# A two-layer decoder trunk on one core: 64 instead of 32 tokens by gathered rows, and two thirds of the key blocks in plain fp32

## The chip, the cores and the metric

One Trainium2 chip, one core. The metric is the device time of one execution in microseconds. Engines: TensorE (PE; its weight loads are PEld), VectorE (DVE), ScalarE (ACT), GpSimd (POOL) and SyncE (SP, which issues most DMAs). Each engine works through its own instructions in program order; semaphores tie them together.

## The reference

Two layers, each a token mixer with cross-attention, a norm, and a channel mixer (PEER) with a norm. All of the change lies in the channel mixer, 256 tokens by 1024 columns in fp32, with 16384 experts a layer:

```python
def block(xb):
    q = (xb @ w_q).reshape(n, PEER_HEADS, 2, PEER_HALF)
    s = jnp.einsum('nhpc,pkc->nhpk', q, sk)
    sv, si = lax.top_k(s, PEER_TOPK)                   # 8 heads, 2 halves, 16 of 128
    cand = sv[:, :, 0, :, None] + sv[:, :, 1, None, :]
    cand_id = si[:, :, 0, :, None] * PEER_KEYS + si[:, :, 1, None, :]
    fv, fi = lax.top_k(cand.reshape(n, PEER_HEADS, -1), PEER_TOPK)
    eid = jnp.take_along_axis(cand_id.reshape(n, PEER_HEADS, -1), fi, axis=-1)
    gw = jax.nn.softmax(fv, axis=-1)
    act = jax.nn.gelu(jnp.einsum('nhkd,nd->nhk', u_tab[eid], xb), approximate=False)
    return jnp.einsum('nhk,nhkd->nd', gw * act, v_tab[eid])
```

So every token uses 128 of the 16384 rows of `u` (keys) and the same 128 rows of `v` (values).

## The kernel before

**Two ways for the tokens.** The first `N` = 224 tokens take the dense way: `u` and `v` are read whole, in 128 blocks each of 128 experts (512 KB), and multiplied by all 224 tokens; the routing weights select. The last `NS` = 32 tokens take the way by rows: their 32 x 128 rows of `u` and of `v` are gathered by indirect DMAs of GpSimd, 128 rows (512 KB) each, 32 for `u` and 32 for `v` a layer.

**Split products.** The accuracy of fp32 is had from the faster form of matmul by splitting each operand into a high part and a rest. `pump` casts a loaded block to `wH` on ScalarE and subtracts it from the block on VectorE or GpSimd to get `wL` (`pool_cols` says how many of the 1024 columns GpSimd takes; `chained` lets it begin after VectorE). Loads go into five raw buffers (`load`), splits into three pairs (`HL_BUFS`). `next` hands out the next block, sees to it that three are split, and lets every generator in `sides` go on by one step (`tick`).

**Key pass** (`peer_layer`). For each of 128 blocks `u_step` issues eight pairs of matmuls: `wH` by [xH | xL] (448 columns) and `wL` by xH (224 columns). ScalarE copies the part of the xL columns out (`low`), and one matmul by the identity adds it (`fold`). Blocks 0 to 63 run beside the routing (`route`, `keys16`, `top16`, `routing`: top 16, softmax, candidate numbers, all on VectorE, spread over the steps by `paced`). In the next 56 steps (`STEPS`), a `scatter` of eight half-precision matmuls spreads the routing weights of four tokens over all experts, from one-hot products that VectorE makes a step ahead (`onehots`); `finish` multiplies them into the GELU of the keys, `wglo` and `wghi`. Then eight blocks without scatter.

**Value pass.** Per block, `coef` splits the weighted GELU into `cc`, and eight pairs of matmuls (448 and 224 columns) add into eight PSUM banks.

**Rows** (`few`, a generator that other loops let go on by one row). For `u`: gather, multiply by the token and sum (`tensor_tensor_reduce`, one number for each row). For `v`: multiply by the coefficient and add to `rep`. Two or three gathers are kept ahead, into three row buffers for `u` and four pieces of `wglo` for `v`. `RATE` is the number of rows let go per value block; at value block `CLOSE` - 2 what is left runs at once and the pool is closed. `grouped` adds the sums to the residual stream.

**Places.** SP's queue carries the loads of blocks; GpSimd's carries the gathers and its share of the splits; ScalarE's carries casts, copies and GELUs; VectorE's carries routing, splits, one-hots, products and rows.

Of the kernel before, what the change touches and what calls it, by code (L numbers as in the profile page):

```python
# [38 lines left out]
NS = 32  # L39
# [3 lines left out]
RATE = 0.6  # L43
CLOSE = 100
# [11 lines left out]
class Trunk:  # L56
# [33 lines left out]
    def pump(self, upto):  # L90
        nc = self.nc
        upto = min(upto, len(self.items))
        while self.n_split < upto:
# [5 lines left out]
            if keep is not None:  # L99
                self.kept[keep] = r  # L100
                continue
            if type(dest) is int:
# [28 lines left out]
    def load(self, upto):  # L131
        while self.n_load < upto:
# [9 lines left out]
            self.n_flight += stage is None  # L142

# [853 lines left out]
    def routing(self, w, tt):  # L997
        nc = self.nc
        sv, si, tmp = self.sv[tt], self.si[tt], self.tmp
        self.pool_cols = D  # L1000
# [15 lines left out]
        self.pool_cols = 0  # L1016
# [59 lines left out]
    def lists(self, w, ef, gw):  # L1076
# [9 lines left out]
        ends = self.sel[:, P - NS:]  # L1086
        nc.vector.tensor_add(ends, self.ident[:, :NS], self.ident[:, NS:2 * NS])
        for k in range(2, GROUPS):
            nc.vector.tensor_add(ends, ends, self.ident[:, k * NS:(k + 1) * NS])
# [5 lines left out]
    def few(self, rows, sums, coefs, old, acc):  # L1095
        nc = self.nc
        rep = self.rep
        for n in range(2):
            self.gather("u_rows", n, rows[n])
            yield  # L1100
        for n in range(NS):
            if n + 2 < NS:
                self.gather("u_rows", n + 2, rows[(n + 2) % 3])
            if NS - 3 <= n < NS:
                self.gather("v", n - NS + 3, old[n - NS + 3])
            r = rows[n % 3]
            nc.vector.tensor_tensor_reduce(r, r, rep, 1.0, 0.0, ALU.mult, ALU.add, sums[:, n:n + 1])  # L1107
            yield
        nc.scalar.activation(sums, sums, AF.Gelu)
        nc.vector.tensor_mul(coefs, sums, self.lot[:, 1])  # L1110
        yield
        for n in range(NS):
            if n + 3 < NS:
                self.gather("v", n + 3, old[(n + 3) % 4])
            r, c = old[n % 4], coefs[:, n:n + 1]
            if n == 0:
                nc.vector.tensor_scalar(rep, r, c, None, op0=ALU.mult)
            else:
                nc.vector.scalar_tensor_tensor(acc[0] if n == NS - 1 else rep, r, c, rep, op0=ALU.mult, op1=ALU.add)  # L1119
            yield  # L1120

# [11 lines left out]
    def u_step(self):  # L1133
        g = self.bank()
        h, l = self.next()
        mm = self.nc.tensor.matmul
# [42 lines left out]
    def peer_layer(self, layer):  # L1179
        nc, tc, A = self.nc, self.tc, self.A  # L1180
        self.layer = layer
        with ExitStack() as ctx:
# [3 lines left out]
            self.sel = wg.tile([P, P], F32, name="sel")  # L1186
            self.lows = ctx.enter_context(tc.tile_pool(name=f"lows{layer}", bufs=1))
            nc.gpsimd.memset(self.sel, 0.0)
            right = ctx.enter_context(ExitStack())
# [4 lines left out]
            rows = [sp.tile([P, D], F32, name=f"row{n}") for n in range(3)]  # L1194
# [3 lines left out]
            flat = lambda t, b: t[:, b:b + 5, :].rearrange("p a b -> p (a b)")[:, :D]  # L1198
            last = []
            few = self.few(rows, sums, coefs, [flat(lo, 5 * n) for n in range(4)], last)  # L1200
# [8 lines left out]
            with ExitStack() as rctx:  # L1209
# [12 lines left out]
                def route():  # L1222
# [13 lines left out]
                    for tt in range(2):  # L1236
                        for q in range(2, 4):
                            self.score(qT, sk, ss[tt], tt, q)
                        yield STEP_US
                    yield from self.keys16(w, 1, ss[1], range(4, 8))  # L1240
                    yield from self.routing(w, 1)
                    first, n = self.ready, 0
                    for side in (self.keys16(w, 0, ss[0], range(4, 8)), self.routing(w, 0)):
                        self.pool_cols = D
                        for c in side:
                            yield c
                            n += 1
                            if n == LATE:
                                first()
                                yield 1.0  # L1250
                    self.pool_cols = POOL_COLS
                    for _ in range(2):
                        next(few)
# [3 lines left out]
                    self.pool_cols = 0  # L1257
                    while self.at < N0 - 3:
                        next(few)
                        yield 1.3  # L1260

                def paced():
                    budget = 0.0
                    for c in route():
                        budget -= c
                        while budget <= 0:
                            yield
                            budget += STEP_US - (0.2 + (D - self.pool_cols) / 960 if self.pool_cols < D else 0)
# [16 lines left out]
                for i in range(N0 + 2):  # L1285
                    self.at = i
                    if i < N0:
                        g.append(self.u_step())
                    if 0 < i <= N0:
# [315 lines left out]
```

## Time and profile before

| | |
|---|---|
| median of three runs | 1772.35 us (1771.82 to 1774.31) |
| profiled execution, own time | 1773.11 us |
| its span, first to last instruction | 1771.3 us |
| granted TensorE clock, mean | 0.991 |
| layer 0, key pass to end of value pass | 186.2 to 888.6 us |
| layer 1, the same | 1046.5 to 1748.9 us |
| DMA moved | 402.91 MB, mean 227 GB/s |
| of it by gathers (queue q0) | 67.12 MB |

A row of the profile names the line of the kernel, the engine, the operation, what it writes and reads, the shapes and a count; then the busy time and the mean of one in ns, and the idle time before it with what ended that. Rows in order of time begin with the start in us from the span's start and the length; several instructions of a kind in a row are merged with a count. Matmuls are pipelined: one lasts longer than the distance to the next, and it is the distance that costs time. A plain fp32 product appears as two matmul records.

### The profile page before, as it was taken

To read this page: it belongs to the slowest core of one execution; us is meant where nothing else is said; L and a number is where in the kernel's file an instruction comes from. 1 tells how busy PE (TensorE), PEld (TensorE's weight loads), DVE (VectorE), ACT (ScalarE), POOL (GpSimd) and SP (SyncE) were. 2 spreads that over 40 slices of the span, in tenths; PEclk is the share of its full clock that TensorE was granted. 3 is DMA by queue.
4 is the path that set the end of the run, shared out by engine and by line. 5 is a ranking of instruction groups with operands and counts; after the bars stand their busy time and mean duration, and the time that the engine had idled before them with its cause. 6 is when DMAs were issued, how large, how long until landed. Compare 5 with 4: busy or idle time off the path is not lost. (4 is left out here: it accounts for less than half of the span.)

```text
span 1771.3 us, 32579 instructions
## 1 busy us (share of the span) xinstructions
PE 1731.4 (98%) x11993; PEld 1639.7 (93%) x11993; DVE 1440.3 (81%) x2847; ACT 1001.6 (57%) x1887; POOL 574.5 (32%) x418
## 2 busy tenths in 40 slices
PE   9999998999999999999999999989999999999997
PEld 9999997999999999999989899979999999999996
DVE  6675589789999888886778756987999988888766
ACT  6554665556655555555658356555665555555554
POOL 3005745133334343330100377223333333333000
PEclk9999999999999999999999999989999999999998
DMA  7655665565557898996746365557555589999763
GB/s 260 199 176 200 191 192 190 179 239 167 167 167 270 299 341 323 334 334 208 280 139 217 119 188 184 187 183 250 169 167 167 182 318 327 344 328 332 261 211 109
DMA packets 115328, 402.91 MB, mean 227 GB/s; under 512 B 13276, under 2 KB 16864, under 8 KB 114912
## 3 DMA queue, kind: packets, MB, share of 16 engines
q1 hardware_dynamic: 94952, 330.30, 56.2%
q0 software_dynamic: 18432, 67.12, 10.0%
q10 hardware_dynamic: 1784, 3.41, 0.6%
q8 instruction: 94, 1.54, 0.3%
q14 instruction: 66, 0.54, 0.1%
HBM read 398.35 MB, written 1.31 MB: 226 GB/s over the span
## 5 line engine op out<-in xcount | busy, mean ns | idle before, releaser
L110 ACT CAST wH<-raw 128x1024 fp32r<-128x1024 f32 (+3 forms) x609 | 628.2, 1033 | 637.8 <-PE bank L1350 276.8
L125 DVE TENSOR_TENSOR wL<-raw,wH 128x1024 fp32r<-128x1024 f32 (+3 forms) x430 | 497.4, 1158 | 244.7 <-ACT wH L110 244.3
L1140 PE MATMUL bank<-xHL,wH 128*128 128x448 f32 x2048 | 668.9, 379 | 0.0
L1350 PE MATMUL bank<-cc,wH 128*128 128x448 f32 x2016 | 632.2, 374 | 2.4 <-DVE wghi L1177 2.4
L1141 PE MATMUL bank<-xHL,wL 128*128 128x224 f32 x2048 | 543.1, 265 | 0.0
L1351 PE MATMUL bank<-cc,wL 128*128 128x224 f32 x2016 | 532.7, 264 | 0.0
L1140 PEld LDWEIGHTS bank<-xHL,wH 128*128 128x128 f32 x2048 | 387.9, 189 | 31.2
L1350 PEld LDWEIGHTS bank<-cc,wH 128*128 128x128 f32 x2016 | 378.0, 188 | 31.6 <-issue 2.9
L1141 PEld LDWEIGHTS bank<-xHL,wL 128*128 128x128 f32 x2048 | 394.3, 193 | 0.0
L1351 PEld LDWEIGHTS bank<-cc,wL 128*128 128x128 f32 x2016 | 384.6, 191 | 0.0
L123 POOL TENSOR_TENSOR wL<-raw,wH 128x1024 fp32r<-128x1024 f32 (+1 forms) x100 | 212.3, 2125 | 233.4 <-ACT wH L110 233.4
L120 POOL TENSOR_TENSOR wL<-raw,wH 128x386 fp32r<-128x386 f32 x112 | 116.1, 1036 | 251.4 <-DVE wL L118 248.6
L1093 POOL DMA_INDIRECT wglo<-in_v_dram,lot x64 | 100.0, 1563 | 166.1 <-DVE rep L1119 132.8
L1093 POOL DMA_INDIRECT row<-in_u_rows_dram,lot x64 | 100.1, 1565 | 138.1 <-DVE sums L1107 136.6
L184 PE MATMUL bank<-xHL,wH 128*128 128x256 f32 x488 | 137.8, 282 | 0.0
L186 PE MATMUL bank<-xHL,wL 128*128 128x256 f32 x488 | 136.5, 280 | 0.2
L185 PE MATMUL bank<-xHL,wH 128*128 128x256 f32 x488 | 135.7, 278 | 0.0
L1127 DVE TENSOR_TENSOR oh<-iota,i12T 128x1024 f16<-128x1024 f16 x112 | 112.3, 1003 | 0.0
L1150 PE MATMUL bank<-low,ident 128*128 128x224 f32 x256 | 80.6, 315 | 18.9 <-ACT low L1146 18.9
L118 DVE TENSOR_TENSOR wL<-raw,wH 128x640 fp32r<-128x640 f32 x112 | 92.4, 825 | 2.7 <-ACT wH L110 2.7
L186 PEld LDWEIGHTS bank<-xHL,wL 128*128 128x128 f32 x488 | 91.9, 188 | 1.1 <-DVE wL L125 0.5
L185 PEld LDWEIGHTS bank<-xHL,wH 128*128 128x128 f32 x488 | 92.3, 189 | 0.3 <-DVE xHL L445 0.2
(340 smaller groups left out, 2211.7 us busy)
## 6 DMA issues: line engine op xcount, KB each, us to landing
raw<-in_u_dram SPq DMA_DIRECT2D x256, 512.0 KB, 3.6
raw<-in_v_dram SPq DMA_DIRECT2D x256, 512.0 KB, 5.2
raw<-in_w_q_dram SPq DMA_DIRECT2D x32, 512.0 KB, 3.8
raw<-in_w_out_dram SPq DMA_DIRECT2D x16, 512.0 KB, 4.4
raw<-in_w0qx_dram SPq DMA_DIRECT2D x8, 512.0 KB, 5.3
raw<-in_w0v_dram SPq DMA_DIRECT2D x8, 384.0 KB, 4.0
raw<-in_w0o_dram SPq DMA_DIRECT2D x8, 384.0 KB, 3.1
raw<-in_w1x_dram SPq DMA_DIRECT2D x8, 384.0 KB, 3.6
```

Of the source, the lines that this page charges most:

```text
L110: (nc.vector.tensor_copy if self.cast_dve else nc.scalar.copy)(h[:, c], r[:, c])
L120: nc.gpsimd.tensor_sub(l[:, :k], r[:, :k], h[:, :k].bitcast(F32))
L123: nc.gpsimd.tensor_sub(l[:, :k], r[:, :k], h[:, :k].bitcast(F32))
L125: rest = lambda l=l, r=r, h=h, c=slice(k, n): nc.vector.tensor_sub(l[:, c], r[:, c], h[:, c].bitcast(F32))
L184: mm(out, sH, mH, start=start, stop=False, skip_group_check=True)
L185: mm(out, sH, mL, start=False, stop=False, skip_group_check=True)
L186: mm(out, sL, mH, start=False, stop=stop, skip_group_check=True)
L1093: self.nc.gpsimd.indirect_dma_start(to, None, rows, bass.IndirectOffsetOnAxis(ap=self.lot[:, 0, n:n + 1].bitcast(I32), axis=0))
L1140: mm(two(g[:, :2 * N]), h[:, c], two(self.xHL[:, dt, :])[:, :, :N], start=dt == 0, stop=False, skip_group_check=True)
L1141: mm(g[:, :N], l[:, c], self.xH[:, dt, :N], start=False, stop=False, skip_group_check=True)
L1350: mm(y[s][:, :2 * N], h[:, c], cc[:, :2 * N], start=i_ == 0, stop=False, skip_group_check=True)
L1351: mm(y[s][:, :N], l[:, c], cc[:, :N], start=False, stop=False, skip_group_check=True)
```

## The change

- `NS` goes from 32 to 64: the dense passes have 192 columns (384 and 192 in a pair), there are 48 scatter steps and 16 key blocks after them, and 64 + 64 gathers a layer.
- `plain`: key blocks 0 to 37 and 64 to 111 of each layer aren't split. `u_step` multiplies the raw block by `xF` = xH + xL in plain fp32; there is no cast, no subtraction, no copy and no fold, and the raw buffer is given back when the products are issued (`spent`).
- GpSimd splits nothing in the key pass; where a block is split there, VectorE does all of it.
- `few` has one ring of four row buffers with three gathers ahead. `deal` lets a row go by a credit: 0.6 a step from the moment that the list is there (first half), 0.85 in the scatter steps, 0.6 after them, 0.55 in the value pass. `CLOSE` is 104.
- `paced` gets its allowance from `room`: 2.5 us a step at plain blocks, less where a block is split, and 0.8 less once rows run.

```diff
-NS = 32
+NS = 64
 N = T - NS
 STEPS = N // 4
 GROUPS = P // NS
-RATE = 0.6
-CLOSE = 100
+CLOSE = 104
+RATES = (0.6, 0.85, 0.6, 0.55)
+ROWS_BUFS = 4
+PLAIN = "plain"
+
+
+def plain(i):
+    return i < 38 or N0 <= i < N0 + STEPS
...
+            if dest is PLAIN:
+                self.split[i] = (r, None)
                 continue
...
+    def spent(self):
+        self.n_flight -= 1
+        self.load(len(self.items))
...
-    def few(self, rows, sums, coefs, old, acc):
+    def few(self, rows, sums, coefs, acc):
         nc = self.nc
-        rep = self.rep
...
+        rep, ring = self.rep, len(rows)
+
+        def fetch(k):
+            if k < 2 * NS:
+                self.gather(("u_rows", "v")[k // NS], k % NS, rows[k % ring])
+        for k in range(ring - 1):
+            fetch(k)
             yield
...
+        for k in range(2 * NS):
+            fetch(k + ring - 1)
+            r, n = rows[k % ring], k % NS
+            if k == NS:
+                nc.scalar.activation(sums, sums, AF.Gelu)
+                nc.vector.tensor_mul(coefs, sums, self.lot[:, 1])
+            c = coefs[:, n:n + 1]
+            if k < NS:
+                nc.vector.tensor_tensor_reduce(r, r, rep, 1.0, 0.0, ALU.mult, ALU.add, sums[:, n:n + 1])
+            elif n == 0:
                 nc.vector.tensor_scalar(rep, r, c, None, op0=ALU.mult)
             else:
                 nc.vector.scalar_tensor_tensor(acc[0] if n == NS - 1 else rep, r, c, rep, op0=ALU.mult, op1=ALU.add)
             yield
+
+    def deal(self, few, rate):
+        self.credit += rate
+        if self.credit >= 1.0:
+            next(few, None)
+            self.credit -= 1.0
...
         h, l = self.next()
+        if l is None:
+            for dt in range(DT):
+                self.fp32(g[:, :N], h[:, dt * P:(dt + 1) * P], self.xF[:, dt], dt == 0, dt == DT - 1)
+            h = None
+            self.spent()
+            return g
...
+                def room():
+                    dest = self.items[self.n_split - 1][2]
+                    if dest is PLAIN:
+                        return 2.5 - 0.8 * self.listed
+                    if self.pool_cols == D:
+                        return STEP_US
+                    return STEP_US - 0.2 - (D - self.pool_cols) / 960 - 0.8 * self.listed
...
                     if i < N0:
                         g.append(self.u_step())
-                    if 0 < i <= N0:
+                        if self.listed:
+                            self.deal(few, RATES[0])
+                    if 0 < i <= N0 and not plain(i - 1):
                         self.fold(g[i - 1], self.low(g[i - 1]))
...
-            self.pool_cols, self.chained = HALF_COLS, True
...
                     if j + 1 < STEPS:
                         oh = self.onehots(j + 1)
-                    elif j >= STEPS:
-                        next(few)
+                    self.deal(few, RATES[1 + (j >= STEPS)])
...
                 if i > 1:
-                    budget += RATE
-                    if budget >= 1.0:
-                        next(few, None)
-                        budget -= 1.0
+                    self.deal(few, RATES[3])
```

The order of instructions, first on TensorE in the key pass of layer 0. Before, the end of one block, its predecessor's fold and the next block (`xHL` holds xH and xL, `low` the copied part, `ident` the identity):

```order
L1140 MATMUL bank<-xHL,wH 128x448
L1141 MATMUL bank<-xHL,wL 128x224
L1150 MATMUL bank<-low,ident 128x224
L1140 MATMUL bank<-xHL,wH 128x448
L1141 MATMUL bank<-xHL,wL 128x224
```

Now, from the last query matmul to the first transposes of the routing (`xF` is the unsplit input, `raw` a loaded block, `sk` and `qT` keys and queries of the routing; one row here is one product, which the chip runs as two records):

```order
L201 MATMUL bank<-xHL,wL 128x256
L272 MATMUL bank<-xF,raw 128x192 x72
L272 MATMUL bank<-sk,qT 128x128 x8
L272 MATMUL bank<-xF,raw 128x192 x8
L272 MATMUL bank<-sk,qT 128x128 x8
L272 MATMUL bank<-xF,raw 128x192 x152
L1076 MATMUL bank<-ident,ef 128x128
```

Eight products stand in the place of sixteen matmuls and a fold, and nothing stands between one block and the next.

On VectorE in the middle of the scatter steps of layer 0, one step before (`wL` the rest of a key block, `wghi` and `wglo` the weighted GELUs, `oh` the one-hot products, `i12T` and `gT` expert numbers and weights):

```order
L118 TENSOR_TENSOR wL<-raw,wH 128x640
L1177 TENSOR_TENSOR wghi<-wghi,bank 128x64
L1165 SCALAR_TENSOR_TENSOR wglo<-bank,wglo 128x64x4
L1167 SCALAR_TENSOR_TENSOR wghi<-bank,wghi 128x17x4
L1127 TENSOR_TENSOR oh<-iota_89,i12T 128x1024
L1130 TENSOR_TENSOR oh<-oh,gT 128x1024
```

and now (`row_1647` is one of the four row buffers; the two rows of line 1122 are one row product and the reading of its sum):

```order
L1196 TENSOR_TENSOR wghi<-wghi,bank 128x80
L1184 SCALAR_TENSOR_TENSOR wglo<-bank,wglo 128x64x4
L1186 SCALAR_TENSOR_TENSOR wghi<-bank,wghi 128x21x4
L1140 TENSOR_TENSOR oh<-iota_89,i12T 128x1024
L1143 TENSOR_TENSOR oh<-oh,gT 128x1024
L1122 ISA row_1647,sums<-row_1647,rep 128x1024
L1122 ISA sums 128x1
```

The split has gone from the step, and in 41 of the 48 steps a row product stands behind the one-hots.

On VectorE near the end of the value pass of layer 0, before, where the last row sum goes into `wghi`:

```order
L254 TENSOR_TENSOR cc<-wghi,cc 128x224
L125 TENSOR_TENSOR wL<-raw,wH 128x1024
L254 TENSOR_TENSOR cc<-wghi,cc 128x224
L1119 SCALAR_TENSOR_TENSOR wghi<-wglo,coefs,rep 128x1024
L125 TENSOR_TENSOR wL<-raw,wH 128x1024
L254 TENSOR_TENSOR cc<-wghi,cc 128x224
```

and now, at value block 102 (`CLOSE` - 2):

```order
L269 TENSOR_TENSOR cc<-wghi,cc 128x192
L136 TENSOR_TENSOR wL<-raw,wH 128x1024
L1126 SCALAR_TENSOR_TENSOR rep<-row_1646,coefs,rep 128x1024
L1126 SCALAR_TENSOR_TENSOR rep<-row_1647,coefs,rep 128x1024
L1126 SCALAR_TENSOR_TENSOR rep<-row_1644,coefs,rep 128x1024
L1126 SCALAR_TENSOR_TENSOR rep<-row_1645,coefs,rep 128x1024
L1126 SCALAR_TENSOR_TENSOR rep<-row_1646,coefs,rep 128x1024
L1126 SCALAR_TENSOR_TENSOR wghi<-row_1647,coefs,rep 128x1024
L269 TENSOR_TENSOR cc<-wghi,cc 128x192
```

Before, the rows were done some blocks ahead of the close; now the last six sums stand together, ahead of the coefficient split of block 104.

More of the change, by code (lines that the diff above doesn't have):

```diff
@@ L1015, in routing @@
                                     for p in range(2)])
-        self.pool_cols = 0
         gw = w.tile([P, 8, 16], F32, name="gw")
@@ L1085, in lists @@
             nc.sync.dma_start(self.lot[k * NS:(k + 1) * NS], pk[rs, k])
[L1086 to L1089, printed above, removed]
     def gather(self, name, n, to):
@@ L1186, in peer_layer @@
             self.sel = wg.tile([P, P], F32, name="sel")
+            wg.tile([P, 8], F32, name="gap")
+            self.xF = wg.tile([P, DT, N], F32, name="xF")
+            self.credit, self.listed = 0.0, False
             self.lows = ctx.enter_context(tc.tile_pool(name=f"lows{layer}", bufs=1))
+            ctx.enter_context(tc.tile_pool(name=f"gap{layer}", bufs=1)).tile([P, 120], F32, name="gap")
             nc.gpsimd.memset(self.sel, 0.0)
+            nc.gpsimd.tensor_add(self.sel[:, P - NS:], self.ident[:, :NS], self.ident[:, NS:])
             right = ctx.enter_context(ExitStack())
@@ L1193, in peer_layer @@
             self.rep = sp.tile([P, D], F32, name="rep")
-            rows = [sp.tile([P, D], F32, name=f"row{n}") for n in range(3)]
+            rows = [sp.tile([P, D], F32, name=f"row{n}") for n in range(ROWS_BUFS)]
             self.lot = sp.tile([P, 2, NS], F32, name="lot")
@@ L1197, in peer_layer @@
             coefs = sp.tile([P, NS], F32, name="coefs")
-            flat = lambda t, b: t[:, b:b + 5, :].rearrange("p a b -> p (a b)")[:, :D]
+            flat = lambda t, b: t[:, b:b + 6, :].rearrange("p a b -> p (a b)")[:, :D]
             last = []
-            few = self.few(rows, sums, coefs, [flat(lo, 5 * n) for n in range(4)], last)
+            few = self.few(rows, sums, coefs, last)
             self.pool_cols = POOL_COLS
@@ L1249, in route @@
                                 first()
+                                self.listed = True
                                 yield 1.0
-                    self.pool_cols = POOL_COLS
-                    for _ in range(2):
-                        next(few)
                     for _ in range(LATE):
@@ L1267, in paced, with whole @@
                             yield
-                            budget += STEP_US - (0.2 + (D - self.pool_cols) / 960 if self.pool_cols < D else 0)
+                            budget += room()
+                def whole():
+                    for _ in range(6):
+                        yield
+                    nc.vector.tensor_add(self.xF, self.xH[:, :, :N].bitcast(F32), self.xL[:, :, :N].bitcast(F32))
+                self.beside(whole())
                 self.asked = False
@@ L1311, in peer_layer @@
                 for j in range(nj - 1):
-                    if j == STEPS:
-                        self.pool_cols, self.chained = 0, False
                     g.append((self.u_step(), scatter() if j < STEPS else None))
-                    if j:
+                    if j and not plain(N0 + j - 1):
                         self.fold(g[j - 1][0], self.low(g[j - 1][0]))
@@ L1320, in peer_layer @@
                         oh = self.onehots(j + 1)
-                    elif j >= STEPS:
-                        next(few)
+                    self.deal(few, RATES[1 + (j >= STEPS)])
             cp = ctx.enter_context(tc.tile_pool(name=f"cp{layer}", bufs=HL_BUFS))
             cp.tile([P, GAP], F32, name="gap", bufs=1)
-            self.pool_cols, self.chained = 0, False
             kept = HL_BUFS - 1
@@ L1485, in tail @@
             for i in range(P):
-                self.add(A["u"][layer, i], D)
+                self.add(A["u"][layer, i], D, PLAIN if plain(i) else None)
             for i in range(P):
```

28 lines of the change are left out of this document (2 added, 26 removed).

## The prediction

> **What bounds the kernel now.** I read the page first, then the busy time by stage, then single rows of each engine in order of time.
>
> ```profile
> PE 1731.4 (98%) x11993; PEld 1639.7 (93%) x11993; DVE 1440.3 (81%) x2847; ACT 1001.6 (57%) x1887; POOL 574.5 (32%) x418
> ```
>
> TensorE is busy almost throughout, so the time is the sum of its passes and of its few waits. The stages of layer 0, cut where the trace shows fold matmuls (columns: stretch, length, busy time of TensorE, weight loads, VectorE, ScalarE, GpSimd, granted clock, DMA share, GB/s):
>
> ```profile
> 191.20:372.50 181.30, 171.88 (x1095) 162.29 (x1093) 145.75 (x476) 105.83 (x199) 82.42 (x39) 0.97 0.63 204
> 372.50:378.80 6.30, 6.26 (x50) 5.78 (x50) 4.88 (x7) 3.20 (x6) 2.15 (x2) 1.00 0.49 114
> 378.80:550.00 171.20, 171.20 (x1356) 158.42 (x1354) 168.26 (x322) 102.94 (x270) 56.41 (x56) 1.00 0.51 169
> 550.00:571.10 21.10, 21.10 (x137) 20.01 (x137) 20.13 (x35) 12.93 (x30) 10.88 (x8) 1.00 0.92 334
> 571.10:888.50 317.40, 316.18 (x2018) 301.53 (x2018) 257.35 (x332) 174.51 (x268) 88.59 (x56) 1.00 0.85 303
> ```
>
> In turn: key blocks 0 to 63 beside the routing ("first half"), the handover, the scatter steps, the key blocks after them, and the value pass. Layer 1 repeats them. VectorE is as full as TensorE in the scatter steps (168.3 of 171.2). A first-half block takes the distance of two folds, 2.64 us:
>
> ```profile
> 204.44 0.28 PE L1150 MATMUL bank<-low,ident 128*128 128x224 f32 x1
> 207.08 0.28 PE L1150 MATMUL bank<-low,ident 128*128 128x224 f32 x1
> ...
> 307.37 0.31 ACT L1020 ACTIVATE gw<-gw 128x128 f32<-128x128 f32 x1 [8.44 <-DVE gw L1019]
> ```
>
> 63 such blocks are 166.3 us; the other 15.0 of the 181.3 are score matmuls and waits. The longest is the last row: ScalarE stands 8.44 us at the softmax's exponential because VectorE is late, and the copy for the next fold is queued behind it.
>
> **Prices on TensorE.**
>
> ```profile
> L257 PE MATMUL bank<-v,pw 128*128 128x193 f32 x24 | 4.1, 326 | 0.0
> ```
> ```profile
> 86.38 3.62 PE L257 MATMUL bank<-pr,vm 128*128 128x256 f32 x16
> 89.83 4.08 PE L257 MATMUL bank<-v,pw 128*128 128x193 f32 x24
> ...
> 94.27 0.33 PE L184 MATMUL bank<-wH,xHL 128*128 128x384 f32 x1
> ...
> 97.39 0.34 PE L184 MATMUL bank<-wH,xHL 128*128 128x384 f32 x1
> ...
> 441.68 0.63 PE L1307 MATMUL bank<-oh 128*128 128x128 f16 x8
> ...
> 442.31 0.37 PE L1140 MATMUL bank<-xHL,wH 128*128 128x448 f32 x1
> ...
> 599.73 0.38 PE L1350 MATMUL bank<-cc,wH 128*128 128x448 f32 x1
> 599.94 0.26 PE L1351 MATMUL bank<-cc,wL 128*128 128x224 f32 x1
> ...
> 602.23 0.38 PE L1350 MATMUL bank<-cc,wH 128*128 128x448 f32 x1
> ```
>
> - Plain fp32: a product is two records. 24 of 193 columns follow each other every (4.08 - 0.33) / 23 = 0.163 us. A **plain block** of eight products at 192 columns is 16 x 0.163 = **2.61 us**, with no fold.
> - Split value block: (602.23 - 599.73) / 8 = 0.3125 us a pair now, 0.21 for the 448 and 0.10 for the 224. The new pair has 384 and 192. From below, 384 columns in a stream of their own take (97.39 - 94.27) / 18 = 0.173, so 0.273 a pair. From above, the 0.21 loses 64 columns at 0.42 ns (193 to 256 columns, 0.163 to 0.216 over 63 columns, is 0.84 ns a column in two passes), about 0.186, and the small matmul, near the pace of its weight load, gains nothing: 0.286. I take 0.284, near the end that comes from this very pattern: **2.27 us a block**.
> - Split key block: its pair is (2.64 - 0.11) / 8 = 0.316; less the same 0.029 and with the fold it is **2.41 us**.
> - Scatter: its eight matmuls and the fold fill 441.68 to 442.31, 0.63 us; without the fold 0.52. A plain block with a scatter needs 3.13 us of TensorE, against 3.17 for the old step.
>
> So a plain block costs TensorE what a split one did (2.61 to 2.64). What it frees is ScalarE and VectorE; TensorE gains from the 42 split key blocks and the 128 value blocks.
>
> **VectorE in a scatter step.**
>
> ```profile
> 441.13 1.07 DVE L1127 TENSOR_TENSOR oh<-iota,i12T 128x1024 f16<-128x1024 f16 x1
> 442.24 0.69 DVE L1130 TENSOR_TENSOR oh<-oh,gT 128x1024 f16<-128x1024 f16 x1
> 442.90 0.83 DVE L118 TENSOR_TENSOR wL<-raw,wH 128x640 fp32r<-128x640 f32 x1
> 443.64 0.23 DVE L1177 TENSOR_TENSOR wghi<-wghi,bank 128x80 f32<-128x80 f32 x1
> 443.81 0.42 DVE L1165 SCALAR_TENSOR_TENSOR wglo<-bank,wglo 128x256 f32<-128x256 f32 x1
> 444.15 0.23 DVE L1167 SCALAR_TENSOR_TENSOR wghi<-bank,wghi 128x84 f32<-128x84 f32 x1
> 444.30 1.07 DVE L1127 TENSOR_TENSOR oh<-iota,i12T 128x1024 f16<-128x1024 f16 x1
> ...
> 354.95 1.21 DVE L125 TENSOR_TENSOR wL<-raw,wH 128x1024 fp32r<-128x1024 f32 x1
> 356.09 1.21 DVE L1107 CUSTOM_DVE_ANT_0 row<-row,rep 128x1024 f32<-128x1024 f32 x1
> ...
> 357.23 1.21 DVE L125 TENSOR_TENSOR wL<-raw,wH 128x1024 fp32r<-128x1024 f32 x1
> ...
> 375.02 0.69 DVE L1127 TENSOR_TENSOR oh<-iota,i12T 128x1024 f16<-128x1024 f16 x1
> 375.74 1.39 DVE L1130 TENSOR_TENSOR oh<-oh,gT 128x1024 f16<-128x1024 f16 x1
> ```
> ```profile
> 355.30 1.68 POOL L1093 DMA_INDIRECT row<-in_u_rows_dram,lot  x1 [0.78 <-DVE sums L1107]
> ...
> 375.24 1.35 POOL L120 TENSOR_TENSOR wL<-raw,wH 128x386 fp32r<-128x386 f32 x1 [9.75 <-DVE wL L118]
> ```
>
> From start to start the old step is 1.11 + 0.66 + 0.74 + 0.17 + 0.34 + 0.15 = 3.17 us, without a gap. The change takes the 0.74 away. It also takes GpSimd's subtraction away, beside which the one-hot products last 1.07 and 1.39 instead of 0.69: -0.39 at the comparison. It adds 0.85 row products of 1.14 (356.09 to 357.23): +0.97, and the growing pieces (80 and 84 columns here) average some 15 columns more, +0.03. That is 3.04 us, beside 3.13 on TensorE: two engines nearly level, and I price the step at the old **3.17**.
>
> The unknown is whether a gather on GpSimd stretches a half-precision product as a subtraction does; no row of before has the two together. Nearest below: the full-precision subtraction at 354.95 ran 1.21 beside the gather at 355.30, as it does elsewhere: nothing. Nearest above: the 1.39, which is +0.70 a gather. I take nothing and keep the other as a rival. [...] The pair at 354.95 and 355.30 speaks against it, the one at 375 for it, and no run here shows the case itself.
>
> **The first half.** 38 plain and 25 split blocks are 38 x 2.61 + 25 x 2.41 = 159.4 us. VectorE there:
>
> ```profile
> L125 DVE TENSOR_TENSOR wL<-raw,wH 128x1024 fp32r<-128x1024 f32 (+1 forms) x47 | 49.0, 1042 | 47.0 <-ACT wH L110 47.0
> ```
>
> It loses these 49.0, gains 26 whole splits (29.6) and 17 row products (19.4): 145.8 us as before, in 166, so it stays covered. A plain block waits for no copy, and from block 38 on VectorE is no longer delayed by GpSimd, so the 8.44 goes. Next late is the exponential of the second routing, in the split blocks. Of the 15.0 I keep 7 (15.0 - 8.44 is 6.6; the bounds are nothing and all 15). Sum 166.4, **-14.9**. The rest of the routing is flushed at block 63 ahead of the first scatter as well, so the handover stays at 6.3.
>
> **The scatter steps and after.** 47 x 3.17 + 16 x 2.41 = 187.6 against 192.3: **-4.7**.
>
> **The value pass.** 126 x 2.27 = 286.0 plus the present 2.4 at its start. VectorE there:
>
> ```profile
> 708.09 0.39 DVE L254 TENSOR_TENSOR cc<-wglo,cc 128x224 fp32r<-128x224 f32 x1
> 708.39 1.28 DVE L1119 SCALAR_TENSOR_TENSOR rep<-wglo,coefs,rep 128x1024 f32<-128x1024 f32 x1
> 709.58 1.22 DVE L125 TENSOR_TENSOR wL<-raw,wH 128x1024 fp32r<-128x1024 f32 x1
> ```
>
> From start to start, with the 1.14 of a whole split (354.95 to 356.09): 1.14 + 0.30 + 0.55 x 1.19 = 2.09 of 2.27, covered by three split buffers. At value block 102 the order shows six row sums together, three of them on rows just asked for, with the coefficient split for block 104 behind them. They take 6 x 1.19 = 7.1 us if the rows are there, some 9 with a landing, and TensorE has two blocks in hand (4.5): I charge 5 (3 to 9). Sum 293.4, **-24.0**.
>
> **Queues.** SP: a plain block's raw buffer comes free when TensorE is done, and the load behind it lands in 3.6 us, with four blocks (10.4 us) until it is needed:
>
> ```profile
> raw<-in_u_dram SPq DMA_DIRECT2D x256, 512.0 KB, 3.6
> ...
> wglo<-in_v_dram,lot POOLq DMA_INDIRECT x64, 7.9
> ```
> ```profile
>   DMA row<-in_u_rows_dram,lot: 3.7, 6
> ```
>
> Hidden. GpSimd's queue holds little else than gathers now; three rows are asked for ahead, 12 us at the value pass's rate, against 7.9 to landing.
>
> **Sum.** -14.9 - 4.7 - 24.0 = -43.6 a layer, -87.2 in all. The profiled execution took 1773.1 us, 0.8 above the median shown; 1773.1 - 87.2 is 1685.9, and I say **1686**.
>
> **Rivals.**
> - *Transfers set the value pass.* 1.55 x 524 KB in 2.27 us is 358 GB/s; the most that a stage shows is 334, at a share of 0.92. For: so near. Against: 334 / 0.92 leaves 363. Held at 334, a block is 2.43 us: +0.16 x 102 x 2 = +33, **1719**.
> - *Gathers stretch the one-hots* by 0.70: VectorE's step is 3.04 + 0.85 x 0.70 = 3.64, +0.47 x 47 x 2 = +44, **1730**. For and against as above.
> - *The pair falls to 0.273*: -0.011 x 8 x 167 x 2 = -29, **1657**.
> - *Slower: VectorE waits for rows.* The queue is in order, so a wait of w us a row holds up the splits and one-hots behind it. Twice as many rows wait in a step that is full: 2 x 47 x (0.85 w - 0.13) + 2 x 102 x (0.55 w - 0.18) = 192 w - 49, with the slack of the two steps above. From w = 0.71 the kernel is slower than before; at 0.8, +105, **1791**. Against: the row above, 3.7 us in 6 waits over 64 rows.
> - *That it doesn't do what it says*: the order has no split for the 86 blocks; nothing is left to chance there.
>
> **Chances.** Forecast 60% (by itself 1668 to 1704), transfers 13%, stretched one-hots 11%, faster pair 12%, row waits 4%. 1652 to 1722 holds the forecast, the faster pair and the transfers and leaves out 15% and the edges. A measurement here tells 0.2%, 3.5 us, from no change: faster 0.95, same 0.01, slower 0.04.
>
> **What would show it.** Plain records every 0.163 us; value pairs at 0.284 (0.273 or over 0.29 is wrong); scatter steps at 3.17, the half-precision products at 0.69; no 8 us wait at the exponential; a hole of about 5 us at value block 102. If TensorE waits on splits in the value pass with the DMA share at its top, the transfers were it; if VectorE waits for rows, the last rival.

## The result and the profile after

| | before | changed |
|---|---|---|
| median of the runs beside each other | 1773.2 us (1771.82 to 1774.31, 4 runs) | 1698.07 us (1694.24 to 1699.42, 4 runs) |
| profiled execution, own time | 1773.11 us | 1694.24 us |
| ratio | | 0.9573, 95% interval 0.9556 to 0.9591 |

The changed kernel is 4.3% faster; 1686 was forecast, with 1652 to 1722 as the range. The direction and the places of the gain were right; by the medians, 12 us of it did not come.

First the two kernels by stage, layer 0, both cut at the same three events: first key matmul, first scatter matmul, first value matmul (columns as in the prediction). Before:

```profile
186.15:375.28 189.13, 179.67 (x1144) 169.57 (x1142) 152.23 (x514) 110.31 (x206) 86.05 (x42) 0.97 0.63 204
375.28:571.15 195.87, 195.87 (x1522) 181.75 (x1520) 191.89 (x361) 117.52 (x301) 69.45 (x64) 1.00 0.56 185
571.15:888.62 317.47, 316.25 (x2019) 301.58 (x2018) 257.42 (x332) 174.63 (x268) 88.54 (x56) 1.00 0.85 303
```

After:

```profile
186.11:362.87 176.76, 171.33 (x1106) 169.81 (x1105) 129.89 (x483) 61.02 (x129) 31.78 (x21) 0.98 0.71 254
362.87:547.98 185.11, 185.11 (x1409) 182.07 (x1407) 175.08 (x368) 60.22 (x193) 55.28 (x50) 1.00 0.90 321
547.98:848.65 300.67, 290.05 (x2020) 288.93 (x2018) 263.88 (x318) 171.03 (x267) 103.26 (x63) 0.98 0.91 331
```

Layer 0 gets shorter by 12.4, 10.8 and 16.8 us: 39.9 together. The scatter stage has no idle time on TensorE at all. The other two have: 5.4 us in the first (176.76 - 171.33) and 10.6 in the value pass, and in both the granted clock is 0.98. Those two places are what the rest of this section and most of the experiments are about. In layer 1 the same cuts give 178.35, 185.11 and 299.31.

The view of waits of the changed kernel (who waited for whom: us in total, times, longest) names both, and answers two questions of the prediction:

```profile
PE bank L1378 <- DVE cc L269: 17.1, 2, 8.7
PE bank L1076 <- DVE ef L1064: 8.2, 2, 4.1
DVE rep L1126 <- DMA row<-in_v_dram,lot: 5.2, 4, 2.0
ACT gw L1033 <- DVE gw L1032: 0.4, 2, 0.2
```

TensorE waits once a layer for a coefficient split (`cc`) in the value pass, up to 8.7 us, and once a layer for the routing's expert numbers (`ef`) at the handover, 4.1 us. VectorE hardly waits for rows, 5.2 us over the 128 rows of `v` of both layers. And the wait at the softmax's exponential, 8.4 us a layer before, is 0.2.

**The prices on TensorE.** Rows in order of time, changed kernel: plain records of nine blocks in a row, one scatter step, and one value block from its first pair to the next one's.

```profile
186.11 23.56 PE L272 MATMUL bank<-xF,raw 128*128 128x192 f32 x144
209.51 1.95 PE L272 MATMUL bank<-sk,qT 128*128 128x128 f32 x16
...
431.82 2.82 PE L272 MATMUL bank<-xF,raw 128*128 128x192 f32 x16
...
434.94 2.82 PE L272 MATMUL bank<-xF,raw 128*128 128x192 f32 x16
```
```profile
700.14 0.36 PE L1378 MATMUL bank<-cc,wH 128*128 128x384 f32 x1
...
702.42 0.36 PE L1378 MATMUL bank<-cc,wH 128*128 128x384 f32 x1
```

144 records in 209.51 - 186.11 = 23.40 us are 0.1625 each, 2.60 a plain block (forecast 2.61). A scatter step is 434.94 - 431.82 = 3.12 us; over the stage it is 3.11 (forecast 3.17). A value block is 702.42 - 700.14 = 2.28, a pair 0.285 (forecast 0.284).

**VectorE in a scatter step**, one step in order of time, and GpSimd's gather beside it:

```profile
431.39 0.23 DVE L1196 TENSOR_TENSOR wghi<-wghi,bank 128x84 f32<-128x84 f32 x1
...
432.03 0.68 DVE L1140 TENSOR_TENSOR oh<-iota,i12T 128x1024 f16<-128x1024 f16 x1
432.75 0.69 DVE L1143 TENSOR_TENSOR oh<-oh,gT 128x1024 f16<-128x1024 f16 x1
433.36 1.22 DVE L1122 CUSTOM_DVE_ANT_0 row<-row,rep 128x1024 f32<-128x1024 f32 x1
434.50 0.08 DVE L1122 DVE_READ_ACCUMULATOR2_ANT sums<- 128x1 f32 x1
```
```profile
431.74 0.94 POOL L1102 DMA_INDIRECT row<-in_u_rows_dram,lot  x1 [2.17 <-DVE wghi L1196]
```

A step with a row is 434.50 - 431.39 = 3.11 us on VectorE, without a gap: exactly TensorE's step. The comparison at 432.03 runs 0.65 us of its 0.68 beside the gather and isn't stretched. The rival of stretched one-hots is out: the view of the one-hot tile gives 694 ns as the longest of 96 comparisons.

**The handover.** TensorE of the changed kernel, from the fold of block 62 to the first scatter, and VectorE before it:

```profile
352.66 0.28 PE L1169 MATMUL bank<-low,ident 128*128 128x192 f32 x1
353.34 0.36 PE L1169 MATMUL bank<-low,ident 128*128 128x192 f32 x1 [0.41 <-ACT low L1165]
357.80 0.45 PE L1076 MATMUL bank<-ident,ef 128*128 128x128 f32 x1 [4.10 <-DVE ef L1064]
...
358.74 4.30 PE L272 MATMUL bank<-xF,raw 128*128 128x192 f32 x16
362.87 0.33 PE L1339 MATMUL bank<-oh 128*128 128x128 f16 x3
```
```profile
349.35 1.47 DVE L1063 TENSOR_TENSOR eq<-eq 128x1024 f16<-128x1024 f16 x3
...
357.36 0.29 DVE L1064 TENSOR_TENSOR ef<-eq 128x128 f32<-128x128 f16 x1
```

From the fold at 352.66 to the scatter it takes 10.2 us. Before:

```profile
371.83 0.28 PE L1150 MATMUL bank<-low,ident 128*128 128x224 f32 x1
...
375.29 0.41 PE L1307 MATMUL bank<-oh 128*128 128x128 f16 x4
```

3.5 us. In the stretch ahead of that fold VectorE is full, 22.52 of 22.66 us (columns as above):

```profile
330.00:352.66 22.66, 22.66 (x163) 22.64 (x161) 22.52 (x30) 11.83 (x27) 10.08 (x6) 1.00 0.94 334
```

VectorE still has eight microseconds of routing, with one row product in it (349.35 to 357.65), when TensorE has no more than 3.3 us of key blocks left. And the plain block behind the wait takes 362.87 - 358.74 = 4.13 instead of 2.60 us.

**The hole at value block 102.** VectorE, with the six row sums, then TensorE:

```profile
784.12 3.92 DVE L1126 SCALAR_TENSOR_TENSOR rep<-row,coefs,rep 128x1024 f32<-128x1024 f32 x3
789.13 1.28 DVE L1126 SCALAR_TENSOR_TENSOR rep<-row,coefs,rep 128x1024 f32<-128x1024 f32 x1 [1.09 <-DMA row<-in_v_dram,lot]
791.49 1.28 DVE L1126 SCALAR_TENSOR_TENSOR rep<-row,coefs,rep 128x1024 f32<-128x1024 f32 x1 [1.08 <-DMA row<-in_v_dram,lot]
793.19 1.28 DVE L1126 SCALAR_TENSOR_TENSOR wghi<-row,coefs,rep 128x1024 f32<-128x1024 f32 x1 [0.42 <-DMA row<-in_v_dram,lot]
794.40 0.35 DVE L269 TENSOR_TENSOR cc<-wghi,cc 128x192 fp32r<-128x192 f32 x1
```
```profile
786.24 0.25 PE L1379 MATMUL bank<-cc,wL 128*128 128x192 f32 x1
794.80 0.69 PE L1378 MATMUL bank<-cc,wH 128*128 128x384 f32 x1 [8.31 <-DVE cc L269]
795.45 0.58 PE L1378 MATMUL bank<-cc,wH 128*128 128x384 f32 x1
...
798.65 0.42 PE L1378 MATMUL bank<-cc,wH 128*128 128x384 f32 x1
```

The sums take 784.12 to 794.40, 10.3 us: 7.7 of work and 2.6 of waiting for rows just asked for. TensorE is out of work at 786.5, 2.4 us after the burst begins: it had one block in hand then, not two. (The split of block 104 stands ahead of the sums in VectorE's queue and takes the buffer pair that block 101 gives back. ScalarE's cast for it begins at 781.89, VectorE's subtraction ends at 784.2, and by then TensorE is at the end of block 102.) And the seven pairs behind the wait take 798.65 - 794.80 = 3.85 us, 0.55 each, where seven pairs at 0.285 are 2.0: another 1.9 us. Half the pace for just under four microseconds after a wait of eight: the granted clock is 0.50 from 794.80 to 798.65, and 0.50 from 357.80 to 361.80 at the handover, and this loss the prediction didn't count. The kernel before has it too, behind the wait at the exponential:

```profile
307.96 0.56 PE L1150 MATMUL bank<-low,ident 128*128 128x224 f32 x1 [8.72 <-ACT low L1146]
```

Its clock is 0.50 from there to 313.50, so with that wait went another 2.7 us. In these traces the waits of 4.1, 8.3 and 8.7 us are followed by half pace, and the 0.41 at the handover isn't (granted clock 1.00 from 353.34 to 353.70). Half pace lasted 4.0 us at the handover, 3.9 at the hole and 5.5 before; it cost 1.9 us at the hole and 2.7 before.

### The profile page after: what moved, and what is told of

It reads as the page before. It is cut to its first block, busy times and chain, and to the rows that moved or that the text cites. A ratio compares the mean times of both kernels' runs of the same rounds, so it can differ in the third digit from the quotient of the medians.

```text
span 1692.5 us, 31388 instructions
## 1 busy us (share of the span) xinstructions
PE 1641.1 (97%) x11693; PEld 1615.8 (95%) x11693; DVE 1393.2 (82%) x2857; ACT 776.5 (46%) x1511; POOL 460.4 (27%) x366
## 5 line engine op out<-in xcount | busy, mean ns | idle before, releaser
L121 ACT CAST wH<-raw 128x1024 fp32r<-128x1024 f32 (+2 forms) x437 | 447.9, 1027 | 418.7 <-PE bank L1378 248.0
L1378 PE MATMUL bank<-cc,wH 128*128 128x384 f32 x2016 | 578.5, 361 | 19.8 <-DVE cc L269 17.1
L1379 PE MATMUL bank<-cc,wL 128*128 128x192 f32 x2016 | 506.5, 251 | 0.8 <-DVE wL L136 0.8
L272 PE MATMUL bank<-xF,raw 128*128 128x192 f32 x2752 | 472.8, 329 | 0.0
L272 PEld LDWEIGHTS bank<-xF,raw 128*128 128x128 f32 x2752 | 448.4, 191 | 0.0
L1102 POOL DMA_INDIRECT row<-in_v_dram,lot x128 | 212.4, 1660 | 328.1 <-DVE rep L1126 295.4
L1159 PE MATMUL bank<-xHL,wH 128*128 128x384 f32 x672 | 198.5, 360 | 0.0
L1160 PE MATMUL bank<-xHL,wL 128*128 128x192 f32 x672 | 168.6, 251 | 0.7 <-DVE wL L136 0.7
L1160 PEld LDWEIGHTS bank<-xHL,wL 128*128 128x128 f32 x672 | 128.3, 191 | 1.0 <-DVE wL L136 1.0
L1159 PEld LDWEIGHTS bank<-xHL,wH 128*128 128x128 f32 x672 | 126.3, 188 | 0.0
L201 PEld LDWEIGHTS bank<-xHL,wL 128*128 128x128 f32 x488 | 92.0, 188 | 0.7 <-DVE wL L136 0.5
```

What stands on the lines that cost most here:

```text
L121: (nc.vector.tensor_copy if self.cast_dve else nc.scalar.copy)(h[:, c], r[:, c])
L201: mm(out, sL, mH, start=False, stop=stop, skip_group_check=True)
L272: self.nc.tensor.matmul(out, lhsT, rhs, start=start, stop=stop, skip_group_check=True)
L1102: self.nc.gpsimd.indirect_dma_start(to, None, rows, bass.IndirectOffsetOnAxis(ap=self.lot[:, 0, n:n + 1].bitcast(I32), axis=0))
L1159: mm(two(g[:, :2 * N]), h[:, c], two(self.xHL[:, dt, :])[:, :, :N], start=dt == 0, stop=False, skip_group_check=True)
L1160: mm(g[:, :N], l[:, c], self.xH[:, dt, :N], start=False, stop=False, skip_group_check=True)
```

## The experiments

All edits are to the changed kernel, 1698.07 us, ratio 0.9573 to the kernel before. Each kernel was timed against the kernel before on its own chip, so ratios are what is compared; where there is only one execution, the stage lengths of its trace are.

### The hole: rows moved into the value pass

```diff
-RATES = (0.6, 0.85, 0.6, 0.55)
+RATES = (0.6, 0.85, 0.6, 0.62)
```

> Value pass at 0.62 instead of 0.55 rows a block: no rows are left for value block 102. Theory (the hole is the six row sums at once, three of them waiting for rows just asked for, and TensorE's half clock behind it): the hole of 8.5 to 9.0 us and the slow block behind it (1.9) go in each layer, about -21 us, to 1677 by the medians; VectorE needs 2.09 + 0.07 x 1.19 = 2.17 of 2.27 us a block. Rival (transfers set the pass once more rows go beside the blocks): the DMA share of the value pass is 0.96 at 352 GB/s, so 367 is the most; 1.62 x 524 KB in 2.275 us is 373 GB/s, a block becomes 2.32 us, some +4 us a layer, to 1685, and TensorE's waits are spread over the pass.

Measured: 1672.01 us (1671.75 to 1672.15), ratio 0.9427 (0.9411 to 0.9443). Its trace has no wait of TensorE for `cc` in the value pass; the two layers' passes are 288.42 and 288.41 us against 300.67 and 299.31, and a block stays at 2.27 to 2.28 throughout. Its DMA traffic in the pass (last two numbers: share and GB/s):

```profile
549.57:780.00 230.43, 229.17 (x1612) 228.90 (x1611) 217.33 (x264) 132.03 (x205) 98.34 (x59) 1.00 0.97 363
```

No wait, and a block at its old length: the rival falls. The 363 GB/s are not above what the prediction (334 / 0.92) and this rival (367) took for the end; whether that is the end, the last experiment shows.

### The hole: rows moved into the scatter steps

```diff
-RATES = (0.6, 0.85, 0.6, 0.55)
+RATES = (0.6, 0.98, 0.6, 0.55)
```

> Scatter steps at 0.98 instead of 0.85 rows: the six rows that were left for value block 102 are done there, the value pass keeps 0.55. Theory (VectorE and TensorE level in the scatter steps): VectorE takes 3.10 to 3.12 us a step, TensorE 3.11, so steps stay within 3.11 to 3.14, and the hole goes: about -19 to -21 us, 1677 to 1679. Rival (VectorE is over the edge when every step has a row, or rows come late there): each step takes 3.25 us or more, +7 us a layer, and 1690 or more.

Measured: 1671.76 us (1671.64 to 1674.66), ratio 0.9426 (0.9410 to 0.9442): the same as by the other way. All steps of the trace lie at 3.11 us. So the hole is the burst, wherever the six rows go instead, and a row in nearly every scatter step is free. (The value pass of layer 0 is 290.08 us here, for 288.42 with the other way; it has a short wait that is named below as left open.)

### The handover: more plain blocks

```diff
-    return i < 38 or N0 <= i < N0 + STEPS
+    return i < 46 or N0 <= i < N0 + STEPS
```

> 46 instead of 38 plain blocks in the first half. Theory (the wait of 4.5 us at the handover, and the slow clock behind it, is VectorE late with the rest of the routing, since the split blocks leave it 0.5 us each): eight blocks free 8 x 1.14 us of VectorE, the wait at the handover falls from 4.5 us to under 1 us, TensorE pays 8 x 0.2 us: net -4 to -6 us a layer, 1686 to 1690 with the hole at value block 102 unchanged. Rival (the wait is a chain of the last routing's own steps, however early it begins): the wait stays, and the kernel is 3 us slower, 1701.

Measured: 1681.29 us (1680.50 to 1684.05), ratio 0.9478 (0.9462 to 0.9494). The first stage is 170.65 us in both layers, 6.1 and 7.7 less. Its handover, TensorE, and VectorE at that time:

```profile
353.61 0.28 PE L1169 MATMUL bank<-low,ident 128*128 128x192 f32 x1
354.29 0.36 PE L1169 MATMUL bank<-low,ident 128*128 128x192 f32 x1 [0.41 <-ACT low L1165]
354.49 0.27 PE L1076 MATMUL bank<-ident,ef 128*128 128x128 f32 x1
...
354.82 2.77 PE L272 MATMUL bank<-xF,raw 128*128 128x192 f32 x16
357.80 0.62 PE L1339 MATMUL bank<-oh 128*128 128x128 f16 x8 [0.22 <-DVE oh L1143]
```
```profile
355.02 0.49 DVE L1080 CAST i12T<-bank 128x128 f16<-128x128 f32 x2 [5.04 <-PE bank L1078]
```

The fold to the scatter is 4.2 us instead of 10.2, the block behind is at full pace, and now it is VectorE that waits, 5.0 us, for TensorE. The lateness was load, not a chain. The medians are 16.8 us apart, 5 more than the most expected; the profiled executions (1684.05, the longest of its four, and 1694.24, the shortest of its four) are 10.2 apart: 13.8 us less in the first stages, 2.3 more in the value passes and 1.3 more elsewhere.

### The handover: fewer rows in place of plain blocks

```diff
-RATES = (0.6, 0.85, 0.6, 0.55)
+RATES = (0.3, 0.98, 0.6, 0.65)
...
-                        return 2.5 - 0.8 * self.listed
+                        return 2.5 - 0.4 * self.listed
...
-                    return STEP_US - 0.2 - (D - self.pool_cols) / 960 - 0.8 * self.listed
+                    return STEP_US - 0.2 - (D - self.pool_cols) / 960 - 0.4 * self.listed
```

> 38 plain blocks in the first half as in the changed kernel, but VectorE relieved otherwise: 0.3 instead of 0.6 rows a step there, and 0.4 instead of 0.8 us kept back for them in the routing's allowance; the rows are made up at 0.98 in the scatter steps and 0.65 in the value pass. Theory (the wait at the handover is VectorE's load in the first half, not the number of plain blocks): some 10 rows of 1.2 us less relieve VectorE by as much as eight plain blocks did, the wait of 4.5 us goes, and TensorE saves 8 x 0.2 us against 46 plain blocks: 1655 to 1658. Rival (only a plain block helps, since in a split block the copy and the fold wait for ScalarE and VectorE anyway): the wait stays over 3 us, 1667 to 1672.

Measured: 1658.15 us (1657.34 to 1658.69), ratio 0.9353 (0.9337 to 0.9369). With 38 plain blocks as in the changed kernel the first stage is 169.98 and 170.68 us: the wait is gone without a further plain block. The edit does two things to VectorE's queue, fewer rows and more room for the routing beside them, and which of the two counts is not shown. The time is at the upper edge of the theory's 1655 to 1658; of the 1.6 us a layer that eight plain blocks fewer should save, layer 0 shows 0.7 and layer 1 nothing. (The hole is gone as well, since no rows are left.)

### Both losses together

```diff
-    return i < 38 or N0 <= i < N0 + STEPS
+    return i < 46 or N0 <= i < N0 + STEPS
...
-RATES = (0.6, 0.85, 0.6, 0.55)
+RATES = (0.6, 0.85, 0.6, 0.62)
```

> 46 plain blocks in the first half and 0.62 rows a value block together. Theory (the two losses, the handover and the hole at value block 102, are apart from each other): the gains add up, 1672.0 less 2 x 6.1 to 7.7 us, 1657 to 1660. Rival (the rows that the shorter first half leaves over come back as a smaller burst at value block 102): 1662 to 1668, with a hole of some us there.

Measured: 1661.01 us, ratio 0.9378 (0.9357 to 0.9398), but from 1658.61 to 1667.63. The profiled execution is the 1658.61: 170.64, 185.11 and 290.06 us by stage in layer 0, no hole. The gains add up there. But the four executions spread over 0.5%, where those of the other kernels stay within 0.3%.

With 42 in place of 46:

> 42 plain blocks in the first half instead of 46, 0.62 rows a value block. Theory (VectorE's lateness at the handover, some 8 us of TensorE's time with the slow clock, shrinks by 1.14 + 0.20 us for each plain block): four blocks take 5.4 us of it, 2 to 3 us of wait stay, TensorE saves 4 x 0.2 us: 1 to 3 us a layer behind the kernel with 46, 1659 to 1665. Rival (four blocks are enough, since VectorE also catches up elsewhere): 1.6 us faster than with 46, 1656 to 1658.

Measured: 1660.29 us (1658.56 to 1663.32), ratio 0.9370 (0.9356 to 0.9383). First stages 171.06 and 170.75 us, 0.1 to 0.4 more than with 46: four blocks were nearly enough, the theory's 2 to 3 us of remaining wait weren't there. The two kernels can't be told apart by time.

With 46, and the rows in the scatter steps, `RATES = (0.6, 0.98, 0.6, 0.55)`:

> 46 plain blocks in the first half, and the six rows done in the scatter steps (0.98) instead of in the value pass (0.55 as in the changed kernel). Theory (a row costs nothing in either place as long as VectorE's step stays under TensorE's, and the gains add up): 1671.8 less 2 x 6.1 to 7.7 us, 1656 to 1660, no hole at value block 102, steps at 3.11. Rival (the kernel with 46 blocks and 0.62 rows ran from 1658.6 to 1667.6, so something in the fuller kernel costs up to 9 us in some executions whatever the place of the rows): the same spread, median 1660 to 1663.

Measured: 1658.94 us (1658.31 to 1660.11, 5 runs), ratio 0.9359 (0.9346 to 0.9372). The theory's number, and a spread of 0.1%: a fuller kernel alone doesn't spread. More rows in the value pass alone don't either: the first experiment has 0.62 and the fewer-rows kernel 0.65, and both are steady. The kernel that spread was run on one chip and these on others, so the chip isn't ruled out. None of the traces is of a long execution, and the cause stays open.

### What the plain blocks are worth: scatter steps split as before

```diff
-    return i < 38 or N0 <= i < N0 + STEPS
+    return i < 38
...
+            self.pool_cols, self.chained = HALF_COLS, True
...
+                    if j == STEPS:
+                        self.pool_cols, self.chained = 0, False
```

> The 48 scatter steps split as before the change (VectorE 640 columns, GpSimd the rest), all else as in the changed kernel. Theory (a plain block is paid for by VectorE, not by TensorE): VectorE's step is 3.0 + 0.74 + 0.39 (one-hots beside GpSimd's subtraction) = 4.1 us, TensorE's 2.40 + 0.63 = 3.0; the step is 4.1 instead of 3.11, +47 us a layer, about 1790. Rival (VectorE isn't what sets the step): 3.0 us a step, -5 us a layer, about 1688.

Measured: 1786.59 us in one execution, 88.5 more than the changed kernel and 0.7% more than the kernel before beside it. The steps with a row are 4.25 to 4.27 us, and the stretch from the first scatter to the last is 190.6 and 191.3 instead of 146.7. VectorE, one step, and the view of the one-hots (shortest, median and longest in ns):

```profile
442.63 1.12 DVE L1140 TENSOR_TENSOR oh<-iota,i12T 128x1024 f16<-128x1024 f16 x1
...
445.54 0.82 DVE L129 TENSOR_TENSOR wL<-raw,wH 128x640 fp32r<-128x640 f32 x1
...
446.90 1.12 DVE L1140 TENSOR_TENSOR oh<-iota,i12T 128x1024 f16<-128x1024 f16 x1
```
```profile
L1140 DVE TENSOR_TENSOR oh<-iota,i12T x96: 678/1066/1332, 362.0 to 1422.1; 128x1024 f16<-128x1024 f16 x96
```

VectorE is full at 446.90 - 442.63 = 4.27 us, and beside GpSimd's subtraction the comparison lasts 1.12 again. So the 64 tokens, with their rows dealt out at these rates, gain nothing without the plain blocks in the scatter steps (other rates weren't tried there). TensorE would have needed less for a split block (2.40 us for 2.60); what the plain blocks give, they give VectorE.

### What the plain blocks are worth: first half split as before

`plain` is true only for the scatter steps, and `pool_cols` is set in the routing as in the kernel before.

```diff
-    return i < 38 or N0 <= i < N0 + STEPS
+    return N0 <= i < N0 + STEPS
```

> The 38 plain blocks of the first half split as before the change, with GpSimd's share there; the scatter steps plain. Theory (the first half is near TensorE's bound either way, so plain blocks there buy the end of the waits and little else): TensorE gains 38 x 0.2 = 7.6 us, the wait at the second softmax of 8 us comes back, the rest of the routing is larger at the handover: -3 to +10 us a layer, 1692 to 1718. Rival (VectorE can't do the splits, the routing and the rows): over +15 us a layer, 1728 or more.

Measured: 1728.15 us in one execution. By the time that is the rival's, by the stages it is between. Its first stage, and two of its waits:

```profile
187.22:374.69 187.47, 168.67 (x1145) 167.55 (x1143) 167.67 (x528) 104.35 (x204) 96.58 (x49) 0.94 0.69 232
```
```profile
PE bank L1382 <- DVE cc L269: 27.2, 2, 13.8
...
ACT gw L1035 <- DVE gw L1034: 23.6, 4, 6.7
```

The first stage is 10.7 us longer in layer 0 (6.4 in layer 1): the waits at the exponential are back, the granted clock of the stage is 0.94 for 0.98, and that costs more than the 7.6 us that TensorE saves. VectorE is fuller too, 167.7 us for 129.9. Of these 37.8 us only 8.7 are more splits of its own (33 for 26). Most of the rest is small instructions of the routing that now stand beside GpSimd's subtractions and last longer; the fourteen sums of candidates of the stage, here and in the changed kernel, show it:

```profile
L1024 DVE TENSOR_TENSOR cand<-sv 128x64 f32<-128x64 f32 (+5 forms) x14 | 18.2, 1370 | 0.0
L1023 DVE TENSOR_TENSOR cand<-sv 128x64 f32<-128x64 f32 (+5 forms) x14 | 2.0, 214 | 0.0
```

In the kernel before they take 8.6 us. So what the plain blocks of the first half take off VectorE is less its own splits than the delay beside GpSimd's. Since the list of rows is ready later (first gather at 290.1 us instead of 270.9, with the stage begun 1.1 later), more rows are left for value block 102, and the hole there grows from 8.7 to 13.8 us. The expectation left out that second effect. There is no wait at the handover, though one was expected.

### Where the transfers end

```diff
-RATES = (0.6, 0.85, 0.6, 0.55)
+RATES = (0.6, 0.85, 0.6, 0.62)
...
+            if self.more is not None and k % 3 == 0 and k + ring - 1 < 2 * NS:
+                self.gather("v", k % NS, self.more)
```

Every third row of the value pass brings one more into a buffer that nothing reads.

> 0.62 rows a value block, and at every third row of the value pass one more row block of v is gathered into a buffer that nothing reads: 0.83 gathers a block, VectorE's work unchanged. Asked for: 1.83 x 524 KB in 2.275 us, 421 GB/s. Theory (a DMA share of 0.95 to 0.96 means that transfers are at their end, 351 / 0.95 = 370 GB/s the most): a block takes 2.59 us while rows last, some +30 us a layer, about 1730. Rival (the share counts the time of packets that wait for each other and isn't the limit; 376 GB/s stood in a slice of the kernel with 0.62): the blocks stay under 2.33 us, 1672 to 1684.

Measured: 1689.27 us in one execution, 17 more than without the extra gathers; neither number. The value passes are 294.37 and 295.02 us, 6 longer than the 288.4, with blocks between 2.27 and 2.60 us. The stretch of the value pass while rows last, and the wait that is new:

```profile
550.21:780.00 229.79, 227.67 (x1574) 223.91 (x1573) 211.14 (x257) 128.32 (x199) 120.33 (x78) 1.00 1.01 398
```
```profile
ACT wH L121 <- DMA raw<-in_v_dram: 139.9, 133, 1.4
```

Now ScalarE's casts wait for loads of `v` 133 times (6 times without the extra gathers), and the traffic is 398 GB/s. That is the end of the transfers in this kernel, and it lies above the 363 and 367 that came of dividing a rate by its share; the changed kernel with its 352 (share 0.96 over its value pass up to the hole) is 12% below it. Some of the 17 us lie outside the value pass and were not followed.

## Why the prediction was right, and where not

It was right by its mechanism and off in three terms, one of which made up for part of the other two. Profiled executions, us a layer, predicted as in the sum; layer 0 and layer 1 measured between the same events:

| stage | predicted | layer 0 | layer 1 |
|---|---|---|---|
| key pass to first scatter | -14.9 | -12.4 | -10.7 |
| scatter steps and after | -4.7 | -10.8 | -10.7 |
| value pass | -24.0 | -16.8 | -18.2 |
| sum | -43.6 | -39.9 | -39.6 |

Twice 39.8, less 0.7 us that the rest of the program took more, are the 78.9 between the profiled executions, where 87.2 was forecast. That the sum came so near is in part luck: the stages of layer 0 are off by 2.5 and 7.2 us one way and by 6.1 the other. The medians are 75 apart, since the profiled execution was the shortest of the four.

- **Right:** the plain block (2.60 for 2.61), the value pair (0.285 for 0.284), the split key block (2.40 for 2.41), VectorE and TensorE level in the scatter steps, the end of the 8.4 us wait at the exponential, the half-precision products unstretched, transfers hidden but for a late load in layer 0 (last point), rows of `v` waited for 5.2 us in all. The pair is right as a sum only: the 384 columns take 0.20 and the 192 take 0.09, for 0.186 and 0.10. No run shows that the small matmul gains nothing beside its weight load; it gained 0.01. None of the rivals came: the row waits, the stretched one-hots and the pair at 0.273 are refuted by rows of the changed kernel, the transfers by its own 352 GB/s at 2.28 us a block and by the kernels at 363 and 398.
- **Failed: "the handover stays at 6.3".** The step looked at what is issued there (the rest of the routing, as before) and not at how much of it is left. VectorE's whole load was taken for the first half, 145.8 of 166 us, and called covered. The total came out smaller, 129.9 us, since the delay beside GpSimd's subtractions went as well, but it is uneven: 51.4 of the 83.9 us until 270, and 22.52 of the 22.66 us ahead of the handover. A split block at the end leaves VectorE some 0.5 us for the routing: 1.14 go to the split and 0.6 rows of 1.2 to the rows, of 2.40. Instead of the wait at the exponential there is one at the handover, 10.2 us for 3.5. What the runs showed in its place: relieve VectorE there, by plain blocks (19.8 of 23.6 us busy in the same stretch) or by fewer rows and more room for the routing (17.9 of 23.0), and the loss goes.
- **Smaller than that loss: the miss of the stage.** It is off by less than the handover's 6.7 us, because the stretch ahead of it came out shorter: of the 7 us that the step kept, 3.9 are the matmuls of the routing's scores, which stayed, but TensorE's idle time up to the fold came to 0.9 us (9.0 before), and the half pace that went with the wait at the exponential wasn't counted. (Two readings of the step are off by little: 40.7 of its 49.0 us of splits lie in the stage, and between the folds that it cuts at lie 62 blocks and a short wait, not 63.) In the other kernels with the same first stage that stage takes 177.8 to 178.8 us, as in layer 1 here; the 176.8 of layer 0 are the exception.
- **Mis-sized: the hole, 5 us (3 to 9).** The burst was right (10.3 us measured, 9 forecast "with a landing"), and so was its place. Two numbers weren't: TensorE had 2.4 us in hand and not 4.5, because the split ahead of the burst waits for a buffer pair of TensorE's, and the half clock behind it, 1.9 us, wasn't counted. It measured 10.4 us in layer 0 and 10.9 in layer 1. The first two experiments, without the burst, got all of it back.
- **Wrong in the other direction: the scatter steps.** The sum has 47 steps besides those in the handover, but from the second scatter to the last there are only 46, which is 3.2 us of the 6; the rest is 3.11 for 3.17. The 3.17 was the old step, VectorE's limit with the split in it; TensorE's 3.13 had been worked out beside it and was the better choice once VectorE's 3.04 lay below.
- **Left open:** 1.5 us at value blocks 115 and 116 of layer 0 that some of the runs show and others don't. ScalarE's cast at 823.30 had waited 3.27 us for a load of `v`; why that load came late isn't known.

The best of the kernels that were run takes 1658.15 us, ratio 0.9353: the change with its rows dealt out so that no burst is left and VectorE is in time at the handover. The one with 46 plain blocks and 0.98 rows a scatter step (0.9359) can't be told from it.

## What to carry to other kernels

A stage's mean load hides where in it the load lies: before calling an engine covered, look at the stretch just ahead of each hand-over, where "what is left" is flushed. Leftover work that is run "at once" on an in-order engine costs its whole length less what the other engine then has in hand (10.3 us less 2.4 at value block 102), and the slow clock after the wait on top (1.9 us); dealing it out at a slightly higher rate was worth 26 us here, a third of the change's own gain. And a form that gains nothing on the fullest engine (plain fp32 on TensorE: 2.60 us a block against 2.40 split) can pay by what it takes off another, and so allow the other half of a change.

## What the runs showed of the hardware

- TensorE ran at half pace for 3.9 to 5.5 us after waits of 4.1, 8.3 and 8.7 us (plain block 4.13 for 2.60 us, value pairs 0.55 for 0.285, granted clock 0.50), and at full pace after one of 0.41 (granted clock 1.00).
- A DMA share of 0.97 was not the end of the transfers: 363 GB/s at that share cost TensorE nothing; at 1.01 it was 398 and loads were waited for.
- A cast of VectorE (128x256) takes 0.29 us in the changed kernel and 2.23 to 2.40 us in the kernel before, where one began at 225.49 beside a subtraction of GpSimd (225.17, 2.41 us long) and ended 0.14 us after it. An indirect gather beside a half-precision product stretched nothing (0.69 us).
- A gather of 128 rows took GpSimd 0.94 us in most scatter steps and 1.68 in most of the value pass. What sets it wasn't tried; it didn't cost time here, since GpSimd is busy 27% of the span.
